# Attention projection of a hybrid decoder step: the branch shares go into the merged tiles ahead of the projection, and the first weight sums move behind the last output block

## The chip, the cores and the metric

One core of a Trainium2 chip runs the whole kernel. The metric is the time on the device in microseconds (us): the median of some runs, and beside it one profiled execution, from which the durations come. Five engines work side by side, each in its own order: PE (TensorE, the matmuls), DVE (VectorE), ACT (ScalarE), POOL (GpSimd) and SP (SyncE, which here only issues DMAs). POOL issues the DMAs that accumulate.

## The reference

One layer of a decoder, for a prompt of 1024 tokens and 8 sample tokens that share the weights. Three branches read the same normalised input, and a gate weighs each of them:

```python
y_a = (sc_b * conv_u) @ w_sc_out
y_b = group_rmsnorm(y_ssd, ssm_norm_w, SSM_GROUPS) @ w_ssm_out
y_c = jnp.einsum('bhlm,bmhd->blhd', probs, mem_v).reshape(bsz, seq, ATTN_DIM) @ w_attn_o
g_a, g_b, g_c = jnp.split(jax.nn.sigmoid(gates), N_BRANCHES, axis=-1)
merged = g_a * y_a + g_b * y_b + g_c * y_c
return merged @ w_merge_o, ...
```

The change concerns the last product of the third branch (`@ w_attn_o`), its gate `g_c`, and the sum `merged`. What follows it is `merged @ w_merge_o`, the residual, and a SwiGLU block.

## The kernel before

Activations lie transposed: a tile has 128 of the 1024 model columns as partitions and the 1032 tokens along its rows. A row of eight such tiles is one activation. Every fp32 product is made of three products of split operands (high by high, high by low, low by high), so every weight block and every activation is first split: ACT casts the high part (`hi`, lines 169, 179, 282, 441), DVE subtracts it from the source for the low part (`lo`, lines 170, 180, 283, 443).

The attention projection works on pairs of output blocks (m = 0, 2, 4, 6; the trace calls them ao0, ao2, ao4, ao6) with a Strassen scheme (`strassen`, line 359). A pair has two raw weight blocks (r1, r2) and seven products of 24 matmuls each (line 295): with the weights A (from r1) the products B11 and B21; with S (sums `sa` of r1 and r2) T1 and nT2; with T (sums `sb`) T3 and B22; with D (the second half of r2) T4. The activations come as seven prepared forms of the attention tiles (`raw8`; names aB11, aT1, ..., aT4; the forms T4 are made last, in `last_aforms`). Three PSUM banks (m0, m1, m2) take the products; ACT copies a result out of its bank (line 380), or DVE combines it with another (lines 351, 429, 431), before the bank is used again. For ao0 and ao2, B11 and B21 are made ahead (`st_head`).

Ahead of the pairs stand the eight output blocks of the second branch (wo20 to wo27, `out_part`, line 1522); the last two are made in halves, and DVE adds to each half a partial sum `yr` loaded by SP (lines 1533, 1543) and multiplies it by its gate (1544). The results go to DRAM as `yg_d` (second branch), and those of the first branch lie in `mg_d`.

In the loop over the pairs (line 1912), `fetch`, called in the middle of `strassen`, loads the gates (line 1925). What is done with the two other shares differs:

- for m = 0 and 2 the gated projection is written to the merged tiles (lines 1941, 1942, 1946), and then four accumulating DMAs of POOL add `yg_d` and, behind these, `mg_d` (line 1952);
- for m = 4 and 6 SP loads `yg_d` into a tile of its own (line 1928), POOL accumulates `mg_d` on it (1929), and DVE adds it to the gated projection (1944, 1945, 1948).

The merged tiles are then split (line 1960) and multiplied by `w_merge_o` (line 2020, tiles `pm`).

The order of the work is made by a planner, which lays the instructions of each engine in a fixed order by the program's order and by what is ready in its own estimate; each engine then works strictly in that order, and waits where something is late. Three devices matter beside that:

- buffers are taken in turn: three for raw weight blocks (tag `raw`), three each for `whi` and `wlo`, five for tiles of the kind `ev` (results, sums, loaded gates), eight for `big` (the attention tiles, then the merged tiles), one for a gate in the pool `fxo`;
- `in_turn` (line 127) keeps the loads of raw blocks, the casts and the subtractions for weights in the program's order;
- `tc.issue_after(x)` keeps an engine's instructions of a block behind x on that engine, without a wait for its end.

Of the kernel before, what the change touches and what calls it, by code (L numbers as in the profile page):

```python
# [9 lines left out]
F32 = mybir.dt.float32  # L10
F32R = mybir.dt.float32r
AF = mybir.ActivationFunctionType
ALU = mybir.AluOpType
# [4 lines left out]
P = 128  # L18
# [3 lines left out]
TT = T + NS  # L22
# [4 lines left out]
KD = D // P  # L27
# [16 lines left out]
def tile_kernel(ctx: ExitStack, tc, a, o):  # L44
    nc = tc.nc
    V, S, G, PE, SY = nc.vector, nc.scalar, nc.gpsimd, nc.tensor, nc.sync

    def f32(t):
        return t.bitcast(F32)
# [21 lines left out]
    def dram(name, shape):  # L71
        return dp.tile(shape, F32, tag=name, name=name)
# [54 lines left out]
    def in_turn(key, ins):  # L127
        if key in prev:
            tc.add_manual_dep(
                ins.ins, prev[key].name,  # L130
                mybir.DependencyInfo(mybir.DependencyClass.NoSync, mybir.DependencyReason.DATA),
                reason="in_turn",
            )
        prev[key] = ins.ins

    loaded = {}

# [35 lines left out]
    def ev_tile(name, shape=(P, TT + 4), dt=F32):  # L173
        return ev.tile(list(shape), dt, tag="ev", name=name)

    def split_act(src, name):
        hi = act_tile("ah", name + "h")
        lo = act_tile("al", name + "l")
        S.copy(hi, src)
        V.tensor_sub(lo, src, f32(hi))  # L180
        return hi, lo
# [67 lines left out]
    def wblock(w, col):  # L249
        return w[:, col : col + P].rearrange("(k p) c -> p k c", p=P)  # L250
# [5 lines left out]
    HS = [slice(0, HT), slice(HT, TT)]  # L256
# [9 lines left out]
    def hv(ps):  # L266
        return ps.rearrange("p n c -> p (n c)")[:, 256 : 256 + HT]

    def halves_of(ps, x, at=0):
        f = hv(ps)  # L270
        for lo, hi in HALF:
            yield f[:, lo:hi], x[:, at + lo : at + hi]

    def st_raw(src, name):
        raw = wp.tile([P, 1024], F32, tag="raw", name=name)
        in_turn("raw", SY.dma_start(raw.rearrange("p (k c) -> p k c", k=KD), src))
        return raw

    def st_split(src, name, n=1024):
        hi = wp.tile([P, 1024], F32R, tag="whi", name=name + "h")  # L280
        lo = wp.tile([P, 1024], F32R, tag="wlo", name=name + "l")
        in_turn("hi", S.copy(hi[:, :n], src))
        in_turn("lo", V.tensor_sub(lo[:, :n], src, f32(hi)[:, :n]))
        return hi, lo

    def st_ps(tag, name):
        return pst[0].tile([P, 2, 512], F32, tag=tag, name=name)

    def st_prod(forms, ps, w, off, f, start):
        for kt in range(4):  # L290
            xh, xl = forms[f][kt]
            ks = slice(off + kt * P, off + (kt + 1) * P)
            for i, (wt, x) in enumerate(((w[0], xh), (w[0], xl), (w[1], xh))):
                for po, xc in halves_of(ps, x):
                    PE.matmul(  # L295
                        po, wt[:, ks], xc, start=(start and kt == 0 and i == 0), stop=(kt == 3 and i == 2),
                        skip_group_check=True,
                    )
# [37 lines left out]
    def st_begin(src1, src2, nm, sums):  # L336
        raw1, raw2 = st_raw(src1, f"{nm}r1"), st_raw(src2, f"{nm}r2")
        wA = st_split(raw1, f"{nm}A")
        sa = sums(f"{nm}sa")
        V.tensor_add(sa[:, :512], raw2[:, :512], raw2[:, 512:])  # L340
        V.tensor_add(sa[:, 512:], sa[:, :512], raw1[:, :512])
        wS = st_split(sa, f"{nm}S")
        return raw1, raw2, sa, wA, wS

    def st_head(wA, forms, nm, o11, tags):

        pa, pc = (st_ps(t, f"{nm}{t}") for t in tags)
        st_prod(forms, pa, wA, 0, "B11", True)
        S.copy(o11, hv(pa))
        st_prod(forms, pc, wA, 512, "B21", True)  # L350
        V.tensor_tensor(o11, hv(pc), o11, op=ALU.add)
        return pa
# [98 lines left out]
    mg_d = dram("mg_d", [KD, P, TT])  # L451
    yr_d = dram("yr_d", [KD, P, TT])
    yg_d = dram("yg_d", [KD, P, TT])
# [34 lines left out]
    with tc.tile_pool(name="p0", bufs=1) as p0, tc.tile_pool(name="pop", bufs=1, space=PSUM) as pop:  # L488
# [30 lines left out]
        for key, src, n in (  # L519
# [13 lines left out]
            while done < n:  # L533
                b, off = divmod(at, P)
                m = min(n - done, P - off)
# [1029 lines left out]
    ins = ((sc_d, a["w_sc_out"][0]), (yb_d, a["w_ssm_out"][0, 0:D]), (yb_d[8:16], a["w_ssm_out"][0, D : 2 * D]), (None, None))  # L1565
# [59 lines left out]
    def big(name):  # L1625
        return ph2[0].tile([P, TT], F32, tag="big", bufs=8, name=name)

    raw8, aforms = [], {}

    def aform(f, kt, src, c=slice(0, HT)):  # L1630
        if kt % 2 == 0 and c.start == 0:
            mk = afx.get(f) or (lambda part, nm: act_tile(part, nm, shape=(P, 2, HT)))
            pair = [mk(part, f"a{f}{kt}{part}") for part in ("ah", "al")]
            aforms.setdefault(f, []).extend(tuple(t[:, i, :] for t in pair) for i in range(2))
        split_to(*(t[:, c] for t in aforms[f][kt]), src)

    afx = {}
    if True:
# [232 lines left out]
            run_next(outs)  # L1871
        wa = [wblock(a["w_attn_o"][0], m * P) for m in range(KD)]
        ev_sums = lambda n: ev_tile(n, (P, 1024))
        begun = st_begin(wa[0], wa[1], "ao0", ev_sums)
        for c in (slice(0, T - HT), slice(T - HT, HT)):
            for kt in range(4):
                b11, b12 = (raw8[kt][:, h][:, c] for h in HS)
# [10 lines left out]
    fxo = fxo_stack.enter_context(tc.tile_pool(name="fxo", bufs=2))  # L1888
    afx["T4"] = lambda part, nm: fxo.tile([P, 2, HT], F32R, tag=part, name=nm)
    oos = [[ev_tile(f"ao0{i}")[:, :TT] for i in range(2)], [ev_tile("ao20")[:, :TT]]]  # L1890
    raw_b = st_raw(wa[2], "ao2r1")
    ta, tb, tc_ = accs
    heads_ = [st_head(begun[3], aforms, "ao0", oos[0][0][:, HS[0]], (ta, tb))]
    wA2 = st_split(raw_b, "ao2A")
    heads_.append(st_head(wA2, aforms, "ao2", oos[1][0][:, HS[0]], (tc_, tb)))

# [6 lines left out]
    def last_aforms():  # L1903
        for kt in range(4):
            aform("B22", kt, raw8[kt + 4][:, HS[1]])
        for kt in range(4):
            t2, b21 = raw8[kt][:, HS[0]], raw8[kt + 4][:, HS[0]]
            V.scalar_tensor_tensor(t2, t2, -1.0, b21, op0=ALU.mult, op1=ALU.subtract)
            aform("T4", kt, t2)

    merged = []
    for m in range(0, KD, 2):
        oo = oos[m // 2] if m < 4 else [big(f"mg{m + i}") for i in range(2)]
        gts, ygs = [], []
        if m == 2:
            oo.append(big("mg3"))
            raw_d = st_raw(wa[3], "ao2r2")
            sa2 = ev_sums("ao2sa")
            V.tensor_add(sa2[:, :512], raw_d[:, :512], raw_d[:, 512:])
            V.tensor_add(sa2[:, 512:], sa2[:, :512], raw_b[:, :512])  # L1920
            begun = raw_b, raw_d, sa2, wA2, st_split(sa2, "ao2S")
        def fetch():
            for i in range(2):
                gts.append((fxo.tile([P, TT], F32, tag="gt", bufs=1, name=f"gt3{m + i}") if i else ev_tile(f"gt3{m + i}"))[:, :TT])
                SY.dma_start(gts[i], gt_d[16 + m + i])
            for i in range(2 if m >= 4 else 0):
                ygs.append(ev_tile(f"yg{m + i}")[:, :TT])
                SY.dma_start(ygs[i], yg_d[m + i])
                G.dma_start(ygs[i], mg_d[m + i], accum_op=ALU.add)

        pa = strassen(
            wa[m], wa[m + 1], aforms, f"ao{m}", ev_sums, lambda: tuple(t[:, c] for t in oo for c in HS),
            begun=begun if m < 4 else None, mid=fetch, hook=None if m else form3,
            after_t3=None if m else last_aforms, head=heads_[m // 2] if m < 4 else None,
        )
        if m == 2:
            accs.clear()
            accs.extend((ta, tb, tc_))
        merged += [big(f"mg{i}") for i in range(2)] if m == 0 else [big("mg2"), oo[1]] if m == 2 else oo
        c1, c0 = HS[1], HS[0]  # L1940
        V.tensor_mul(merged[m], oo[0], gts[0])
        V.tensor_mul(merged[m + 1][:, c1], oo[1][:, c1], gts[1][:, c1])
        if m >= 4:
            V.tensor_add(merged[m], merged[m], ygs[0])
            V.tensor_add(merged[m + 1][:, c1], merged[m + 1][:, c1], ygs[1][:, c1])
        V.scalar_tensor_tensor(merged[m + 1][:, c0], pa, -1.0, gts[1][:, c0], op0=ALU.mult, op1=ALU.mult)
        if m >= 4:
            V.tensor_add(merged[m + 1][:, c0], merged[m + 1][:, c0], ygs[1][:, c0])
        else:
            for src in (yg_d, mg_d):  # L1950
                for i in range(2):
                    G.dma_start(merged[m + i], src[m + i], accum_op=ALU.add)
    fxo_stack.close()
    aux_stack = ExitStack()
    auxp = aux_stack.enter_context(tc.tile_pool(name="aux", bufs=3))
# [4 lines left out]
    mg = [split_act(merged[m], f"mgs{m}") for m in range(KD)]  # L1960
# [164 lines left out]
    for n, (j, j2) in enumerate(pairs):  # L2125
        s1, s2, pa = hidden_pair("g", j, j2)
# [3 lines left out]
        u1, u2, pa = hidden_pair("u", j, j2)  # L2130
# [73 lines left out]
    for part, js in enumerate(([0], [9, 10])):  # L2204
# [6 lines left out]
        begun = st_begin(*down_src(part, 0), f"d{part}0", ev_sums)  # L2211
# [199 lines left out]
```

## Time and profile before

| | us |
|---|---|
| median of 3 runs | 2439.47 (2437.26 to 2442.43) |
| the profiled execution | 2439.55 |
| its span, first to last instruction | 2437.8 |
| PE busy | 2393.3 (98%) |
| DVE busy | 1644.2 (67%) |
| ACT busy | 1113.0 (46%) |
| POOL busy | 116.3 (5%) |

The attention projection begins about 1545 us after the span's start and ends at 1654.45, where the merge product begins. A row of the timeline gives start, duration, engine, line, operation, result and operands, and in brackets how long the engine had been idle before and what released it. A row of the waits gives who waited for whom, the total, the number of times and the longest. A row of a stretch gives the busy time of each engine in it, with the number of instructions, PE's granted clock and how busy the 16 DMA engines were. The trace leaves out buffer numbers, so `mg` is any merged tile, and `yr` any of its kind.

### The profile page before, as it was taken

The page shows a single profiled execution, that of the slowest core. Times are in us where ns is not written, and L with a number is a line of the kernel's source. Part 1 is how long each engine was busy: PE and PEld are TensorE (multiplying, and loading weights), DVE is VectorE, ACT ScalarE, POOL GpSimd, SP SyncE. Part 2 cuts the span into 40 slices and gives each one's busy share as a digit, 9 for nine tenths or more (in the row PEclk, how much of TensorE's full clock was granted, in tenths as well). Part 3 has the DMA queues.
Part 4 walks back from the last instruction along what each step waited for, and adds up shares of the span by engine and source line. Part 5 has one row for each costly group of instructions (what it writes and reads, how often), then busy time and mean ns, then how long its engine had stood idle before and what let it go on. Part 6 is the DMA issues. An engine that isn't in the chain of part 4 may idle for free. (4 is left out here: it accounts for less than half of the span.)

```text
span 2437.8 us, 45645 instructions
## 1 busy us (share of the span) xinstructions
PE 2393.3 (98%) x18860; PEld 2285.6 (94%) x18860; DVE 1644.2 (67%) x2686; ACT 1113.0 (46%) x1792; POOL 116.3 (5%) x175
## 2 busy tenths in 40 slices
PE   8999999999999999999999999889999999999998
PEld 6999999999999999888888887889999999999998
DVE  6744676777777775568687763755777655567965
ACT  6634555455454544656555442333553333343423
POOL 0000000000000000212211000010000000000000
PEclk9999999999999999999999999999999999999999
DMA  6444423444444346669787887496455332355622
GB/s 212 134 155 158 131 89 113 130 139 131 130 151 119 113 122 191 205 226 291 243 292 212 274 316 265 146 224 196 134 178 171 105 109 94 103 169 159 195 85 81
DMA packets 356678, 407.90 MB, mean 167 GB/s; under 512 B 15230, under 2 KB 276462, under 8 KB 356463
## 3 DMA queue, kind: packets, MB, share of 16 engines
q1 hardware_dynamic: 331606, 335.39, 44.8%
q10 hardware_dynamic: 23137, 63.26, 6.8%
q0 software_dynamic: 1728, 6.34, 1.4%
q8 instruction: 148, 2.42, 0.4%
q14 instruction: 59, 0.48, 0.1%
HBM read 288.81 MB, written 116.35 MB: 166 GB/s over the span
## 5 line engine op out<-in xcount | busy, mean ns | idle before, releaser
L1055 ACT ACTIVATE r<-r,acum 128x128 f32<-128x128 f32 x256 | 79.3, 391 | 3.4 <-DMA r<-ac_d 2.5
L844 DVE SCALAR_TENSOR_TENSOR ax<-u,prm,ax 128x1024 f32<-128x1024 f32 x44 | 56.3, 1279 | 0.0
L996 ACT ACTIVATE st<-st,es 128x128 f32<-128x128 f32 x128 | 41.4, 392 | 20.9 <-DMA st<-in_state_ssm_dram 13.5
L1088 POOL TENSOR_TENSOR xdd<-xdt,decst 128x512 f32<-128x512 f32 x32 | 35.2, 1101 | 284.9 <-DVE xdt L1084 279.0
L1082 DVE TENSOR_TENSOR r<-r,cbm 128x1024 f32<-128x1024 f32 x32 | 39.1, 1222 | 4.3 <-ACT r L1057 2.4
L998 DVE SCALAR_TENSOR_TENSOR st<-sr,dts,st 128x128 f32<-128x128 f32 x128 | 40.3, 345 | 0.4
L1107 DVE TENSOR_TENSOR y<-po,ea 128x512 f32<-128x512 f32 x28 | 19.3, 689 | 31.2 <-PE po L1103 31.2
L1124 PE MATMUL pss<-xdd,bT 128*128 128x512 f32 x64 | 34.4, 619 | 2.0 <-ACT bT L1081 1.4
L1002 DVE SCALAR_TENSOR_TENSOR sr<-st,sr 128x128 f32<-128x128 f32 x128 | 35.3, 286 | 1.1
L1111 PE MATMUL py<-r,xdt 128*64 128x128 f32 x512 | 35.0, 279 | 0.0
L1057 ACT ACTIVATE r<-r 128x1024 f32<-128x1024 f32 x32 | 33.8, 1058 | 0.7
L1137 POOL TENSOR_TENSOR s<-s,cdec 128x512 f32<-128x512 f32 x28 | 33.1, 1184 | 0.8 <-DVE s L1130 0.6
L2034 DVE TENSOR_TENSOR x<-pm,xT 128x516 f32<-128x516 f32 x15 | 10.4, 693 | 32.2 <-PE pm L2020 31.2
L1111 PEld LDWEIGHTS py<-r,xdt 128*64 128x64 f32 x512 | 27.3, 136 | 4.4 <-issue 1.0
L1103 PE MATMUL po<-bc,s 128*128 128x128 f32 x224 | 29.6, 275 | 0.0
L1103 PEld LDWEIGHTS po<-bc,s 128*128 128x128 f32 x224 | 28.0, 191 | 1.0
L1689 ACT ACTIVATE pr<-psa,mx 128x256 f32<-128x256 f32 x32 | 14.9, 469 | 29.5 <-DVE mx L1687 29.5
L847 DVE SCALAR_TENSOR_TENSOR ax<-u,prm,ax 128x1032 f32<-128x1032 f32 x22 | 28.3, 1286 | 0.0
L1677 DVE SCALAR_TENSOR_TENSOR kc<-kc,qb 128x256 f32<-128x256 f32 x64 | 23.8, 419 | 6.4 <-DMA qb<-qs_d 6.4
L841 ACT ACTIVATE ax<-u,prm 128x1024 f32<-128x1024 f32 x22 | 27.4, 1246 | 1.2 <-ACT u L923 0.4
L1084 DVE TENSOR_TENSOR xdt<-xp,dtT 128x512 f32<-128x512 f32 x32 | 21.9, 684 | 8.4 <-PE xp L1077 8.4
L1081 ACT COPY bT<-bp 128x128 f32<-128x128 f32 x32 | 8.3, 261 | 38.5 <-DVE cbm L1079 38.5
(9294 smaller groups left out, 9055.9 us busy)
## 6 DMA issues: line engine op xcount, KB each, us to landing
r<-ac_d SPq DMA_DIRECT2D x32, 512.0 KB
gt_d<-G ACTq DMA_DIRECT2D x24, 516.0 KB
gt<-gt_d SPq DMA_DIRECT2D x24, 516.0 KB
xs_d<-ax ACTq DMA_DIRECT2D x22, 516.0 KB
zs<-zs_d SPq DMA_DIRECT2D x16, 516.0 KB
yb_d<-x SPq DMA_DIRECT2D x16, 516.0 KB
in<-yb_d SPq DMA_DIRECT2D x16, 516.0 KB
st<-in_state_ssm_dram SPq DMA_DIRECT2D x32, 256.0 KB
```

Source lines behind the costliest of these rows:

```text
L844: V.scalar_tensor_tensor(acc[:, :T], u[:, j : j + T], w[j], acc[:, :T], op0=ALU.mult, op1=ALU.add)
L996: S.activation(st[:, i], st[:, i], AF.Copy, scale=es[:, g * 4 + i, b : b + 1])
L998: V.scalar_tensor_tensor(st[:, i], rb, dts[:, g * 4 + i, b : b + 1], st[:, i], op0=ALU.mult, op1=ALU.add)
L1002: V.scalar_tensor_tensor(rb, st[:, i], 1.0, rc, op0=ALU.mult, op1=ALU.mult, accum_out=ys[:, g * 4 + i, b : b + 1],)
L1055: S.activation(r[:, j, :], r[:, j, :], AF.Relu, scale=-1.0, bias=acum[:, c, h : h + 1])
L1057: S.activation(r, r, AF.Exp, scale=-1.0)
L1082: V.tensor_tensor(r, r, bc(cbm.unsqueeze(1), [P, HPG, P]), op=ALU.mult)
L1088: G.tensor_tensor(b3(xdd, HPG), b3(xdt, HPG), bc(decst[:, c, hs].unsqueeze(2), [P, HPG, 64]), op=ALU.mult)
L1103: PE.matmul(po[:, t * P : (t + 1) * P], state["s"][:, t * P : (t + 1) * P], bcg[1][:, cs], start=True, stop=True,)
L1111: PE.matmul(py[hp : hp + 64, (h // 2) * P : (h // 2 + 1) * P], xdt[:, h * 64 : (h + 1) * 64], r[:, (h % 2) * 4 + h // 2, :], start=True, s ...
L1124: PE.matmul(pss, bT, xdd, start=True, stop=True)
L1137: G.tensor_tensor(b3(s_new, HPG), b3(state["s"], HPG), bc(cdec[:, c, hs].unsqueeze(2), [P, HPG, 64]), op=ALU.mult,)
```

## The change

The first pair's start is divided. Ahead of the last output block only r1 of ao0 is loaded and split; r2 is loaded behind that block, and its sums S follow the two heads. Result tiles of all pairs are now `ev` tiles, and the merged tiles are made in `shares`: SP loads `yg_d` into the merged tile, POOL accumulates `mg_d` on it. For m = 0 that is called when the last forms are done, for the other pairs in `fetch`; on SP it is kept behind the latest load of a raw weight block. DVE then multiplies the result by its gate in place and adds it to the merged tile, for all four pairs. The two gates of a pair change places between `ev` and `fxo`.

```diff
         prev[key] = ins.ins
+        return ins.ins
...
+    last_raw = [None]
+
     def st_raw(src, name):
         raw = wp.tile([P, 1024], F32, tag="raw", name=name)
-        in_turn("raw", SY.dma_start(raw.rearrange("p (k c) -> p k c", k=KD), src))
+        last_raw[0] = in_turn("raw", SY.dma_start(raw.rearrange("p (k c) -> p k c", k=KD), src))
         return raw
...
-        begun = st_begin(wa[0], wa[1], "ao0", ev_sums)
+        raw_a = st_raw(wa[0], "ao0r1")
+        wA0 = st_split(raw_a, "ao0A")
...
+    raw_c = st_raw(wa[1], "ao0r2")
     raw_b = st_raw(wa[2], "ao2r1")
     ta, tb, tc_ = accs
-    heads_ = [st_head(begun[3], aforms, "ao0", oos[0][0][:, HS[0]], (ta, tb))]
+    heads_ = [st_head(wA0, aforms, "ao0", oos[0][0][:, HS[0]], (ta, tb))]
...
+    def sums_of(raw1, raw2, nm):
+        sa = ev_sums(f"{nm}sa")
+        V.tensor_add(sa[:, :512], raw2[:, :512], raw2[:, 512:])
+        V.tensor_add(sa[:, 512:], sa[:, :512], raw1[:, :512])
+        return sa, st_split(sa, f"{nm}S")
+
+    def shares(ms):
+        for m in ms:
+            merged.append(big(f"mg{m}"))
+            with tc.issue_after(last_raw[0]):
+                SY.dma_start(merged[m], yg_d[m])
+            G.dma_start(merged[m], mg_d[m], accum_op=ALU.add)
+
+    def last_forms_and_shares():
+        last_aforms()
+        shares(range(2))
+
     for m in range(0, KD, 2):
-        oo = oos[m // 2] if m < 4 else [big(f"mg{m + i}") for i in range(2)]
-        gts, ygs = [], []
-        if m == 2:
-            oo.append(big("mg3"))
+        gts = []
+        if m == 0:
+            oo = oos[0]
+            sa0, wS0 = sums_of(raw_a, raw_c, "ao0")
+            begun = raw_a, raw_c, sa0, wA0, wS0
+        elif m == 2:
+            oo = oos[1] + [ev_tile("ao21")[:, :TT]]
             raw_d = st_raw(wa[3], "ao2r2")
-            sa2 = ev_sums("ao2sa")
-            V.tensor_add(sa2[:, :512], raw_d[:, :512], raw_d[:, 512:])
-            V.tensor_add(sa2[:, 512:], sa2[:, :512], raw_b[:, :512])
-            begun = raw_b, raw_d, sa2, wA2, st_split(sa2, "ao2S")
+            sa2, wS2 = sums_of(raw_b, raw_d, "ao2")
+            begun = raw_b, raw_d, sa2, wA2, wS2
+        else:
+            oo = [ev_tile(f"ao{m}{i}")[:, :TT] for i in range(2)]
+            begun = None
+
         def fetch():
             for i in range(2):
-                gts.append((fxo.tile([P, TT], F32, tag="gt", bufs=1, name=f"gt3{m + i}") if i else ev_tile(f"gt3{m + i}"))[:, :TT])
+                gts.append((ev_tile(f"gt3{m + i}") if i else fxo.tile([P, TT], F32, tag="gt", bufs=1, name=f"gt3{m + i}"))[:, :TT])
                 SY.dma_start(gts[i], gt_d[16 + m + i])
-            for i in range(2 if m >= 4 else 0):
-                ygs.append(ev_tile(f"yg{m + i}")[:, :TT])
-                SY.dma_start(ygs[i], yg_d[m + i])
-                G.dma_start(ygs[i], mg_d[m + i], accum_op=ALU.add)
+            if m:
+                shares(range(m, m + 2))
...
-            begun=begun if m < 4 else None, mid=fetch, hook=None if m else form3,
-            after_t3=None if m else last_aforms, head=heads_[m // 2] if m < 4 else None,
+            begun=begun, mid=fetch, hook=None if m else form3,
+            after_t3=None if m else last_forms_and_shares, head=heads_[m // 2] if m < 4 else None,
...
-        merged += [big(f"mg{i}") for i in range(2)] if m == 0 else [big("mg2"), oo[1]] if m == 2 else oo
         c1, c0 = HS[1], HS[0]
-        V.tensor_mul(merged[m], oo[0], gts[0])
-        V.tensor_mul(merged[m + 1][:, c1], oo[1][:, c1], gts[1][:, c1])
-        if m >= 4:
-            V.tensor_add(merged[m], merged[m], ygs[0])
-            V.tensor_add(merged[m + 1][:, c1], merged[m + 1][:, c1], ygs[1][:, c1])
-        V.scalar_tensor_tensor(merged[m + 1][:, c0], pa, -1.0, gts[1][:, c0], op0=ALU.mult, op1=ALU.mult)
-        if m >= 4:
-            V.tensor_add(merged[m + 1][:, c0], merged[m + 1][:, c0], ygs[1][:, c0])
-        else:
-            for src in (yg_d, mg_d):
-                for i in range(2):
-                    G.dma_start(merged[m + i], src[m + i], accum_op=ALU.add)
+        V.tensor_mul(oo[0], oo[0], gts[0])
+        V.tensor_add(merged[m], merged[m], oo[0])
+        V.tensor_mul(oo[1][:, c1], oo[1][:, c1], gts[1][:, c1])
+        V.tensor_add(merged[m + 1][:, c1], merged[m + 1][:, c1], oo[1][:, c1])
+        V.scalar_tensor_tensor(oo[1][:, c0], pa, -1.0, gts[1][:, c0], op0=ALU.mult, op1=ALU.mult)
+        V.tensor_add(merged[m + 1][:, c0], merged[m + 1][:, c0], oo[1][:, c0])
```

## The prediction

> **What bounds the kernel now.** I read the page first, then PE's waits around the attention projection (the four pairs ao0, ao2, ao4, ao6), then the stretches there, and at last each engine's timeline and the queues.
>
> ```profile
> span 2437.8 us, 45645 instructions
> PE 2393.3 (98%) x18860; PEld 2285.6 (94%) x18860; DVE 1644.2 (67%) x2686; ACT 1113.0 (46%) x1792; POOL 116.3 (5%) x175
> ...
> PE ao0m L295 <- DVE yr L1543: 6.0, 2, 5.7
> PE ao2m L295 <- DVE mg L429: 5.6, 1, 5.6
> PE ao6m L295 <- DVE ao6Sl L283: 1.6, 1, 1.6
> PE ao6m L295 <- DVE mg L431: 1.3, 1, 1.3
> ```
>
> PE is the bound nearly everywhere, so only a hole in PE's work can be won. The region has three, which I call A (5.7 us, ahead of ao0), B (5.6 us, in ao2) and C (1.3 and 1.6 us, in ao6). The stretches show what else is full there; the columns after the times are PE, PEld, DVE, ACT and POOL busy, PE's granted clock, the DMA share and GB/s.
>
> ```profile
> 1570.00:1580.00 10.00, 10.00 (x86) 10.00 (x85) 10.00 (x17) 5.80 (x9) 0.00 (x0) 1.00 0.33 107
> 1580.00:1590.00 10.00, 10.00 (x86) 10.00 (x85) 7.83 (x11) 2.54 (x4) 1.89 (x2) 1.00 0.48 118
> 1590.00:1600.00 10.00, 8.49 (x70) 8.09 (x68) 1.62 (x3) 2.11 (x4) 1.72 (x2) 1.00 1.05 247
> 1600.00:1610.00 10.00, 5.91 (x30) 5.91 (x31) 8.15 (x11) 1.76 (x2) 0.85 (x1) 0.66 1.05 274
> ```
>
> VectorE is full up to about 1588 while the DMA engines are half empty; then they are full, VectorE sits idle and PE stops. Hole B, on VectorE, the SP queue and POOL:
>
> ```profile
> 1588.43 0.38 SPq L276 DMA_DIRECT2D ao4r<-in_w_attn_o_dram x1
> 1586.55 1.01 POOL L1952 DMA_DIRECT2D mg<-yg_d  x1 [279.17 <-DVE mg L1941]
> 1595.62 0.86 POOL L1952 DMA_DIRECT2D mg<-mg_d  x1 [6.33 <-DMA mg<-yg_d]
> DMA to landing us min/median/max: 7.7/9.1/9.8
> 1599.80 0.69 DVE L398 TENSOR_TENSOR ao4sa<-ao4r 128x512 f32<-128x512 f32 x1 [8.38 <-DMA ao4r<-in_w_attn_o_dram]
> 1603.35 0.68 DVE L429 TENSOR_TENSOR mg<-mg,ao2m 128x516 f32<-128x516 f32 x1
> 1604.09 0.80 PE L295 MATMUL ao2m<-aT40ah,ao2Dh 128*128 128x256 f32 x2 [5.60 <-DVE mg L429]
> ```
>
> The second weight block of ao4 is asked for at 1588.43, among the accumulating DMAs of mg0 and mg1, and arrives at 1599.8, 11.4 us later. VectorE works in order: L398 waits for that block, and L429, which clears the bank PE needs for T4, stands five instructions behind it. Hole C is of the same kind, with an accumulate as the late one:
>
> ```profile
> 1606.66 0.81 SPq L1928 DMA_DIRECT2D yg<-yg_d x2
> 1611.17 1.11 POOL L1929 DMA_DIRECT2D yg<-mg_d  x1
> 1620.58 1.18 POOL L1929 DMA_DIRECT2D yg<-mg_d  x1
> 1632.24 0.70 DVE L1945 TENSOR_TENSOR mg<-mg,yg 128x516 f32<-128x516 f32 x1 [6.96 <-DMA yg<-mg_d]
> ```
>
> The share of yg5 is issued on POOL only at 1620.58, after the chained accumulates of mg2 and mg3, and L1945 holds VectorE for 6.96 us.
>
> **What the holes are worth.** PE's rows at the borders of the pairs:
>
> ```profile
> 1609.35 0.40 PE L295 MATMUL ao4m<-aB110ah,ao4Ah 128*128 128x256 f32 x2
> 1629.36 0.40 PE L295 MATMUL ao6m<-aB110ah,ao6Ah 128*128 128x256 f32 x2
> 1636.59 0.64 PE L295 MATMUL ao6m<-aT10al,ao6Sh 128*128 128x256 f32 x2
> 1654.45 25.59 PE pm L2020 x213
> ```
>
> The undisturbed pair ao4 takes 1629.36 - 1609.35 = 20.0 us for seven products, 2.86 each. The pair ao6 takes 1654.45 - 1629.36 = 25.1, so C costs 5.1: 2.9 of waiting and 2.2 at the lower clock behind it. In B, T4 runs from 1604.09 to 1609.35, 5.3 us instead of 2.9: B costs 5.6 + 2.4 = 8.0. Here a rule and a row differ. The row at 1636.59 shows a pair of matmuls at 0.64 us, not 0.40, although neither wait of C exceeds 1.6 us. "TensorE: Matmul & The Clock Gate" in the Trainium skill (Part 1, What's actually happening) has the clock fall after an idle window of about 3.4 us; by that, C would be worth 2.9 alone and the ceiling below 2.2 smaller. The row decides, and it also says that a new hole of 2 or 3 us costs about 2.2 more than itself.
>
> **The change, part by part.** *The second ao0 block and its sums move behind the last output block.* Weight splits keep the program's order (in_turn): now the split of the output block wo27 comes behind that of ao0S, which waits for the block ao0r2. With ao0S moved, wo27's split is free to run early.
>
> ```profile
> 1551.52 1.22 DVE L170 TENSOR_TENSOR wo27l<-wo27r,wo27h 128x1024 fp32r<-128x1024 f32 x1
> 1544.45 1.29 DVE L1543 TENSOR_TENSOR yr<-po,yr 128x516 f32<-128x516 f32 x2 [13.92 <-issue]
> 1545.80 0.58 PE L295 MATMUL ao0m<-aB110ah,ao0Ah 128*128 128x256 f32 x1 [5.71 <-DVE yr L1543]
> 1539.66 0.43 SPq L1533 DMA_DIRECT2D yr<-yr_d x1
> ```
>
> PE can then take wo27 straight after wo26. Its first half has an empty bank, its second needs the first of the two L1543, done at about 1545.1. So A stays: it hangs on the yr load issued at 1539.66, which is not touched, and PE gains 0.7 us at most (1545.8 against 1545.1), nothing if the order stays. The block ao0r2, its two adds (0.68 each) and split (1.22) have the whole of wo27 and two heads (four products, 11.4 us) before T1 wants them. They cost nothing while that cover holds; without it their 2.6 us plus a cast of 1 us would stand in front of T1.
>
> *The merged shares.* Twelve accumulating DMAs become eight and four plain loads become eight; the bytes stay. In the window 1540 to 1680 the two queues show:
>
> ```profile
> q1 hardware_dynamic: 20112, 19.52, 45.0%
> q0 software_dynamic: 1728, 6.34, 24.1%
> ```
>
> An accumulate fills all engines for 24.1% of 140 / 12 = 2.8 us, a plain 0.53 MB load for 45.0% of 140, by 19.52 MB, x 0.53 = 1.7. The queues lose 4 x 1.1 = 4.4 us of work. More matters when they start: the merged tiles are free as soon as the last forms have read the attention tiles.
>
> ```profile
> 1574.96 0.68 DVE L443 TENSOR_TENSOR aT40al<-at,aT40ah 128x516 fp32r<-128x516 f32 x1
> 1584.76 1.23 DVE L1941 TENSOR_TENSOR mg<-ao,gt 128x1032 f32<-128x1032 f32 x1
> 1585.91 0.69 DVE L1942 TENSOR_TENSOR mg<-ao,gt 128x516 f32<-128x516 f32 x1
> 1587.72 0.68 DVE L328 SCALAR_TENSOR_TENSOR ao2sb<-ao2sa,ao2r 128x512 f32<-128x512 f32 x1
> 1589.60 1.22 DVE L283 TENSOR_TENSOR ao2Tl<-ao2sb,ao2Th 128x1024 fp32r<-128x1024 f32 x1 [1.19 <-ACT ao2Th L282]
> 1592.39 0.40 PE L295 MATMUL ao2m<-aB220ah,ao2Th 128*128 128x256 f32 x2
> 1635.86 1.23 DVE L1944 TENSOR_TENSOR mg<-mg,yg 128x1032 f32<-128x1032 f32 x1
> ```
>
> So yg0 and yg1 can be asked for at about 1576, ten microseconds before the first accumulate of now, into queues a third full. For ao4 and ao6 the shares no longer wait for an ev buffer (1606.66 above) nor behind mg2 and mg3 on POOL. C's cause goes: I take its 5.1 back in full, with 0 as the other end should VectorE still meet a late share.
>
> For B, the accumulates of mg0 and mg1 are done or nearly so when ao4r2 is asked for, and mg2 and mg3 no longer form chains of two. Four accumulates at 2.8 us are 11.2 us of engine work; if half of them are over by 1588, the 11.4 us of ao4r2 fall by up to 5.6, and with the shorter wait the clock may hold. I take 6 of B's 8.0; the ends are 0 (the same bytes in the way) and 8.0.
>
> *What VectorE gets more.* ao0 and ao2 gain an add of 1.23 and two of 0.69 each, 2.6 us a pair. In ao2 they meet time in which VectorE idles (8.38). In ao0 it has none, and ao2Tl ends at 1590.8 for a product starting at 1592.39: a margin of 1.6 us. wo27l (1.22) leaves this stretch for idle time. Also the adds now wait for the shares: yg0 asked for at 1576, landed 3.9 us later (SP's 1606.66 to POOL's move on at 1610.55 is such a load), plus 9.1 for the accumulate, gives 1589, where VectorE could add at 1586. If the program's order holds, ao2sb and ao2T stand 3 us plus the adds behind that, ao2Tl ends about 4 us later, PE waits some 3 us and loses 2.2 of clock, 5 together; if the planner lets ao2sb pass, nothing. Ends 0 and 5; I take 3, between them since I cannot see the new order.
>
> **Sum.** 0.7 + 5.1 + 6 - 3 = 8.8 us off the profiled run. That run took 2439.55 (1.75 beside its span), 0.1 from the median of 2439.47, so I forecast 2430.7. What a measurement of this kernel can tell from no change is about 0.2%, 4.9 us.
>
> **Rivals.** *All is won:* no new wait and B closed: 0.7 + 5.1 + 8.0 = 13.8, 2425.7. For it speaks the idle DMA time before 1586, against it VectorE's full rows to 1588.
>
> *Hole B stays.* The weight block still shares the engines with POOL's accumulates, since the new order only holds back SP's loads: only C and the start are won and the 3 us paid, 2.8 off, 2436.7. The rows of 1586.55 to 1595.62 speak for it: four accumulates flew while SP's block took 11.4 us. "DMA: Bandwidth & Descriptors" of the Trainium skill (Issuing engines are not separate DMA queues) says that transfers of all issuing engines interleave on the same 16 engines. By that an order on SP alone does not protect the block; the 11.4 us agree.
>
> *Slower: the shares become VectorE's bound.* Place: the first add of ao0, with ao2sb behind it. When the last share of ao0 lands at time L, what follows is an add, the product with its add, two ao2sb sums, the cast and the split, some 5.6 us, so PE gets ao2T at L + 5.6 and loses L + 5.6 - 1591.7 plus 2.2. It eats the 13.8 at L = 1597.7; if B stays as well, the 5.8 left is eaten at 1589.7. L would be that late if yg1 were asked for only at 1587, behind a load on SP that waits for its buffer (3.9 + 9.1 = 13.0). At L = 1600 and B staying, the loss is 16.1 against 5.8: 10.3 slower, 2449.9. Against it: the SP rows show transfers of later pairs issued when ready, not held behind earlier blocked ones.
>
> *The change doesn't do what it says:* the planner asks for the shares no earlier than today's accumulates, holes as before, the adds in their shadow: 2439.5.
>
> **How the numbers follow.** Forecast 0.4, all won 0.17, B stays 0.15, inert 0.08, slower 0.2. Faster by over 0.2% (below 2434.6): the first two and a little of the third, 0.6. Within 0.2%: the rest of the third, inert and the mild end of slower, 0.2. Slower by over 0.2%: 0.2, the slower rival and combinations of it, less its mild end. The range runs from all won with 1.7 to spare, 2424.0, to 2445.0, half way into the slower rival.
>
> **What would show it.** Right: plain loads of yg_d on SP into mg at about 1576; the first accumulate on POOL before 1582; no 5.6 us wait of PE at T4 of ao2, none at T1 of ao6; wo27 on PE ahead of ao0's B11. Wrong: PE's waits naming ao2Tl or an mg add, VectorE idle for "mg<-mg_d", or ao4r still 11 us under way. The merge products (pm) should start about 9 us earlier than 1654.45.

## The result, and the profile after

The changed kernel takes 2436.06 us, median of 20 runs (2431.87 to 2439.0), against 2440.01 of the kernel before on the same chips (20 runs, 2436.99 to 2445.74). The ratio is 0.9981, interval 0.9974 to 0.9988: about 4.6 us faster, where 8.8 were forecast. The profiled execution took 2438.7.

PE's waits from 1530 to 1700 us, changed kernel (the wait ahead of wo26, the same in both kernels, left out):

```profile
PE ao2m L298 <- ACT ao2Sh L285: 9.9, 1, 9.9
...
PE ao0m L298 <- ACT ao0Sh L285: 1.0, 1, 1.0
PE ao0m L298 <- DVE yr L1546: 0.7, 1, 0.7
PE ao0m L298 <- DVE ao0Sl L286: 0.6, 1, 0.6
PE ao2m L298 <- DVE ao L354: 0.5, 1, 0.5
PE ao2m L298 <- DVE ao2Al L286: 0.4, 1, 0.4
```

The long waits of before are gone: 5.7 at yr (A), 5.6 in ao2 (B), 1.3 and 1.6 in ao6 (C). In their place stands one new wait of 9.9 us, for the weights ao2S, and a row of short ones. The borders of the blocks and pairs on PE's timeline, first in the kernel before, then in the changed one:

```profile
1526.89 0.50 PE L242 MATMUL po<-b00h,wo26h 128*128 128x256 f32 x2 [1.32 <-DVE yr L1558]
...
1586.68 0.41 PE L295 MATMUL ao2m<-aT10ah,ao2Sh 128*128 128x256 f32 x2
...
1654.29 0.40 PE L2020 MATMUL pm<-mgs0h,wm00h 128*128 128x256 f32 x2
```

```profile
1530.34 0.51 PE L243 MATMUL po<-b00h,wo26h 128*128 128x256 f32 x2 [1.32 <-DVE yr L1561]
...
1543.38 0.40 PE L243 MATMUL po<-b00h,wo27h 128*128 128x256 f32 x2
1549.07 0.40 PE L243 MATMUL po<-b00h,wo27h 128*128 128x256 f32 x2
...
1612.12 0.40 PE L298 MATMUL ao4m<-aB110ah,ao4Ah 128*128 128x256 f32 x2
...
1632.08 0.40 PE L298 MATMUL ao6m<-aB110ah,ao6Ah 128*128 128x256 f32 x2
...
1652.04 0.40 PE L2039 MATMUL pm<-mgs0h,wm00h 128*128 128x256 f32 x2
```

The changed kernel's first row starts 3.45 us later than that of the kernel before. The instructions ahead of it are the same in the same order, so that is the variation of one execution, and what follows is measured by the **region**: from the first matmul of wo26 to the first of the merge product. It is 127.4 us before (1526.89 to 1654.29) and 121.7 after, 5.7 less. The pair ao6 takes 19.96 us, as undisturbed as ao4: C is gone. At 1543.38 the first half of wo27 runs straight behind wo26, in an empty bank, and the second half follows without a wait: that is how A went.

Where the new wait comes from, on the timelines of SP, POOL, DVE and PE:

```profile
1577.65 2.14 SPq L1928 DMA_DIRECT2D mg<-yg_d  x4
1581.86 1.01 POOL L1929 DMA_DIRECT2D mg<-mg_d  x1 [273.15 <-DVE ao L432]
1583.09 0.87 POOL L1929 DMA_DIRECT2D mg<-mg_d  x1 [0.23 <-DVE aT42al L446]
1585.63 0.68 DVE L1920 TENSOR_TENSOR ao2sa<-ao2r 128x512 f32<-128x512 f32 x1
1588.72 1.23 DVE L1967 TENSOR_TENSOR mg<-mg,ao 128x1032 f32<-128x1032 f32 x1 [2.40 <-DMA mg<-mg_d]
1592.85 0.69 DVE L1969 TENSOR_TENSOR mg<-mg,ao 128x516 f32<-128x516 f32 x1 [2.90 <-DMA mg<-mg_d]
1593.46 0.69 DVE L1970 SCALAR_TENSOR_TENSOR ao<-ao0m,gt 128x516 f32<-128x516 f32 x1
1594.07 0.68 DVE L1921 TENSOR_TENSOR ao2sa<-ao2sa,ao2r 128x512 f32<-128x512 f32 x1
1595.93 0.80 PE L298 MATMUL ao2m<-aT10ah,ao2Sh 128*128 128x256 f32 x2 [9.86 <-ACT ao2Sh L285]
```

The sum ao2sa has two instructions. The first, L1920, ran at 1585.63. Between it and the second, L1921, the planner has put both adds of ao0 that need shares (L1967, L1969) and L1970, which needs the end of T4 of ao0. The shares came 6.9 and 9.8 us after POOL had asked for them, VectorE waited 2.40 and 2.90 us, and PE, which wanted T1 of ao2 at 1586.07, got it at 1595.93.

The block behind hole B, by contrast, came quickly:

```profile
1597.06 0.68 DVE L331 SCALAR_TENSOR_TENSOR ao2sb<-ao2sa,ao2r 128x512 f32<-128x512 f32 x1
1597.77 0.38 SPq L279 DMA_DIRECT2D ao4r<-in_w_attn_o_dram  x1
1602.47 0.69 DVE L401 TENSOR_TENSOR ao4sa<-ao4r 128x512 f32<-128x512 f32 x1 [1.72 <-DMA ao4r<-in_w_attn_o_dram]
```

That is 4.7 us against 11.4 before. But it was also asked for late: 11.7 us behind the point at which PE could have begun T1 of ao2 (1586.07), where it was 1.7 us in the kernel before (1588.43 and 1586.68). With three buffers in turn, this block takes the one of ao2's first block, whose last reader is the second sum T (L328 before, L331 now); in every traced run the request goes out 0.7 us after that sum's start. The new wait held that sum up. By 1597.77 the accumulates of mg0 to mg2 had landed, and that of mg3 had 0.8 us to go (asked for at 1586.43, 12.1 us under way).

### The profile page after: what moved, and what is told of

It reads as the page before. It is cut to its first block, busy times and chain, and to the rows that moved or that the text cites. A ratio compares the mean times of both kernels' runs of the same rounds, so it can differ in the third digit from the quotient of the medians.

```text
span 2437.0 us, 45647 instructions
## 1 busy us (share of the span) xinstructions
PE 2388.5 (98%) x18860; PEld 2281.0 (94%) x18860; DVE 1647.6 (68%) x2692; ACT 1112.9 (46%) x1792; POOL 112.9 (5%) x171
## 5 line engine op out<-in xcount | busy, mean ns | idle before, releaser
L999 ACT ACTIVATE st<-st,es 128x128 f32<-128x128 f32 x128 | 41.3, 392 | 18.4 <-DMA st<-in_state_ssm_dram 16.2
L2053 DVE TENSOR_TENSOR x<-pm,xT 128x516 f32<-128x516 f32 x15 | 10.4, 693 | 32.0 <-PE pm L2039 32.0
```

The lines of the kernel that those rows point to most:

```text
L999: S.activation(st[:, i], st[:, i], AF.Copy, scale=es[:, g * 4 + i, b : b + 1])
```

## The experiments

Region is from the one profiled execution of each kernel, ratio from the timed runs against the kernel before on the same chip, with its 95% interval.

| kernel | region, us | ratio | longest hole of PE |
|---|---|---|---|
| before | 127.4 | 1 | A, B, C |
| changed | 121.7 | 0.9981 (0.9974 to 0.9988) | T1 of ao2, 9.9 |
| block alone | 125.1 | 0.9991 (0.9981 to 1.0001) | T4 of ao2, 3.1; T1 of ao2, 2.6 |
| shares alone | 123.3 | 0.9987 (0.9978 to 0.9996) | T1 of ao2, 6.1; A, 6.0 |
| pair 0 as before | 128.0 | 1.0004 (0.9995 to 1.0014) | T4 of ao2, 10.5 |
| one share left out | 117.2 | 0.9963 (0.9951 to 0.9975) | T1 of ao2, 5.0 |
| no order on SP | 126.0 | 1.0012 (0.9997 to 1.0026) | T1 of ao2, 10.7 |
| pair 2 held | 122.7 | 0.9980 (0.9969 to 0.9990) | T1 of ao2, 10.5 |
| sums S first | 120.0 | 0.9975 (0.9964 to 0.9985) | T3 of ao2, 6.8 |
| sums S first, pair 2 held | 122.8 | 0.9978 (0.9969 to 0.9987) | T3 of ao2, 6.4 |
| all sums first | 123.0 | 0.9978 (0.9970 to 0.9987) | T3 of ao2, 9.4 |
| and ao4's blocks first | 117.0 | 0.9962 (0.9949 to 0.9975) | T3 of ao2, 3.3 |
| and a cast behind a copy | 119.9 | 0.9968 (0.9957 to 0.9979) | T3 of ao4, 4.7 |

The theory: from about 1579 to 1605 the DMA engines are full but for a dip about 1598, and PE stops where an engine that works in order has something that PE needs behind an instruction that waits for a transfer. The rival: VectorE is full, and the order of its work alone makes the hole. The fences of the experiments hold rows of the timelines of PE, VectorE and, where they matter, SP, POOL and ScalarE, each of the kernel that its paragraph is about.

**The moved block alone** (kernel before, with only the second ao0 block and its sums moved):

```diff
-        begun = st_begin(wa[0], wa[1], "ao0", ev_sums)
+        raw_a = st_raw(wa[0], "ao0r1")
+        wA0 = st_split(raw_a, "ao0A")
...
+    raw_c = st_raw(wa[1], "ao0r2")
```

> The kernel before with only the second ao0 block and its sums moved behind the last output block; shares as before. Theory 1 (the shares make the new hole: DVE waits for them with ao2's sums behind it): hole A goes (8.0 us with its clock), B (8.0) and C (5.1) stay, no hole at T1 of ao2; 8 us faster, ratio 0.9967. Rival (the new order alone makes it: ao2's second sum stands behind the gated product that needs T4 of ao0): a hole of some 4 us and 2 us of clock at T1 of ao2 with no share waited for; 2 us faster, ratio 0.999.

```profile
1560.32 0.47 PE L295 MATMUL ao0m<-aB210ah,ao0Ah 128*128 128x256 f32 x2 [0.73 <-DVE yr L1543]
1591.28 0.80 PE L295 MATMUL ao2m<-aT10ah,ao2Sh 128*128 128x256 f32 x2 [2.63 <-ACT ao2Sh L282]
1607.59 0.60 PE L295 MATMUL ao2m<-aT40ah,ao2Dh 128*128 128x256 f32 x2 [3.13 <-DVE mg L429]
```

A is closed by the block alone, since of the wait for yr 0.73 us is left. B is there, shorter because PE, held at T1, comes to T4 later. And T1 of ao2 waits 2.63 us though VectorE waits for no share here: the rival holds for that part, and its ratio of 0.999 is the one measured.

**The shares alone** (changed kernel, ao0's block and sums ahead as before):

```diff
-        raw_a = st_raw(wa[0], "ao0r1")
-        wA0 = st_split(raw_a, "ao0A")
+        begun = st_begin(wa[0], wa[1], "ao0", ev_sums)
```

> The kernel after with both ao0 blocks and their sums ahead of the last output block, as before; shares as after. Theory 1: A stays, B and C go (13.1), but the adds of ao0 wait for the shares and hold ao2's weights as in the kernel after, 12 us; 1 us faster, ratio 0.9996. Rival: ao2's sums come early in this order, so there is no hole at T1; the adds hold ao2sb at most, 3 to 5 us and 2 of clock at T3; 6 to 8 us faster, ratio 0.997.

```profile
1595.74 0.77 PE L298 MATMUL ao2m<-aT10ah,ao2Sh 128*128 128x256 f32 x2 [6.06 <-DVE ao L434]
1594.30 0.70 DVE L1965 TENSOR_TENSOR mg<-mg,ao 128x516 f32<-128x516 f32 x1 [5.33 <-DMA mg<-mg_d]
```

A stays, B and C go. The hole at T1 of ao2 is there as well, by another road: ao2S is ready, but the bank is cleared by L434, which stands behind the add that waits 5.33 us for a share. The hole is half of what the theory expected, where the rival expected none.

**Pair 0 added by DMA as before** (changed kernel otherwise):

```diff
         last_aforms()
-        shares(range(2))
...
+        if m == 0:
...
+                    G.dma_start(merged[i], src[i], accum_op=ALU.add)
```

> The kernel after with the pair ao0 added as before (gated product written to the merged tiles, four accumulating DMAs behind it), the other three pairs by shares. Theory 1: no DVE instruction waits for a share in ao0; what is left at T1 of ao2 is the wait for T4, 4 us and 2 of clock; if hole B stays closed, 8 us faster than before more than after gives: 21 less 6 less 3 = 12 faster, ratio 0.995; if the accumulates of ao0 beside ao4's block open B again (8 us), 4 faster, ratio 0.998. Rival: the hole at T1 of ao2 stays near 10 us, ratio 0.998 or above.

```profile
1586.43 0.50 PE L298 MATMUL ao2m<-aT10ah,ao2Sh 128*128 128x256 f32 x2 [2.63 <-ACT ao2Sh L285]
1586.47 0.38 SPq L279 DMA_DIRECT2D ao4r<-in_w_attn_o_dram  x1
1607.40 0.69 DVE L401 TENSOR_TENSOR ao4sa<-ao4r 128x512 f32<-128x512 f32 x1 [17.93 <-DMA ao4r<-in_w_attn_o_dram]
1610.60 0.80 PE L298 MATMUL ao2m<-aT40ah,ao2Dh 128*128 128x256 f32 x2 [10.47 <-DVE ao L432]
```

Without adds that wait for shares, T1 of ao2 waits 2.63 us, as with the block alone. The large hole is B again: ao4's second block is 20.9 us under way, where it meets four accumulates and the early shares of pair 2. This run does not tell which of two differences closes B in the changed kernel, the early shares of pair 0 or the late request: here the block is also asked for only 2.7 us behind the point at which PE could begin T1 of ao2, not 11.7. The run with all sums first, below, bears on that.

**One share left out.**

```diff
-            G.dma_start(merged[m], mg_d[m], accum_op=ALU.add)
+            m < 2 or G.dma_start(merged[m], mg_d[m], accum_op=ALU.add)
```

> The changed kernel without the two accumulating DMAs of the first branch on mg0 and mg1; that share is missing from those two merged tiles. VectorE's order is the changed kernel's but for two swaps of an add with a sum. Theory (VectorE's adds wait for shares that the DMA engines bring late, and ao2's second sum stands behind them): no wait of VectorE for a share in pair ao0, the hole at T1 of ao2 falls from 9.9 us to the 2.6 us that the order alone cost when only the block was moved, so some 7 us less, about 2429 us. Rival (the hole is VectorE's load and order, the shares only happen to land then): the hole stays over 7 us, 2435 to 2437 us.

```profile
1593.11 0.80 PE L298 MATMUL ao2m<-aT10ah,ao2Sh 128*128 128x256 f32 x2 [4.98 <-ACT ao2Sh L285]
```

No add waits for a share, and the hole is 4.98 us: between the two expectations. The 2.4 us above the 2.6 of order (the block alone) come with the new adds and two swaps in VectorE's order. Most of the 9.9 us of the changed kernel can be told from its own rows: the two adds ahead of L1921 take some 1.8, and VectorE waits 2.40 and 2.90 for transfers; with the 2.6 of order, which another kernel showed, that is 9.7.

**No order on SP** (the loads of shares not kept behind the last raw block; only SP's order differs):

```diff
-            with tc.issue_after(last_raw[0]):
+            with nullcontext():
```

> The changed kernel without keeping the share loads behind the last raw weight block on SP; only SP's order differs: the loads for mg4 to mg7 stand ahead of the second weight block of ao4. Theory (queue order on SP protects that block): the block is up to 3.4 us (two plain loads at 1.7) later than its 4.7 us, or SP itself is held by tiles that are not free and asks for the block late; a hole at T4 of ao2 comes back, 2438 to 2445 us. Rival (transfers go out as their tiles come free, whatever SP's order, and the clause does nothing): 2435.5 to 2436.5 us.

```profile
1585.28 5.67 SPq L1928 DMA_DIRECT2D mg<-yg_d  x4
1597.71 0.38 SPq L279 DMA_DIRECT2D ao4r<-in_w_attn_o_dram  x1
1609.04 0.69 DVE L401 TENSOR_TENSOR ao4sa<-ao4r 128x512 f32<-128x512 f32 x1 [8.34 <-DMA ao4r<-in_w_attn_o_dram]
1612.25 0.50 PE L298 MATMUL ao2m<-aT40ah,ao2Dh 128*128 128x256 f32 x2 [1.69 <-DVE ao L432]
```

The clause matters: without it the shares of pairs 4 and 6 go out ahead of ao4's second block, which, asked for at nearly the same time, then takes 11.3 us instead of 4.7, and no gain is left in the timed runs: the theory's range of 2438 to 2445 holds with 2444.5. These twelve runs spread from 2437.4 to 2453.5 us, and the traced one took 2440.4, so the trace shows less than the median has lost. I had held that an order on SP alone does not protect the block.

**Pair 2's shares held back** behind the load of gt32 (only SP's order differs):

```diff
-                SY.dma_start(gts[i], gt_d[16 + m + i])
+                last_raw[m != 2 or i] = SY.dma_start(gts[i], gt_d[16 + m + i]).ins
```

> The changed kernel; SP's loads of the second branch's share for mg2 and mg3 kept behind the load of the gate gt32, nothing else in any engine's order differs. Theory (the DMA engines' queue sets the landing: two plain loads of 1.7 us and then two accumulates of 2.8 us stand in the way of mg0 and mg1): the share of mg1 lands 3 to 4 us earlier, the hole at T1 of ao2 falls from 9.9 to about 6 us, 2432 to 2433 us. Rival (the same bytes only meet another reader): the held shares now fly with the second weight block of ao4 and its wait comes back as a hole at T4 of ao2; 2436 to 2439 us.

```profile
1595.08 0.86 POOL L1929 DMA_DIRECT2D mg<-mg_d  x1 [11.35 <-DVE ao L1970]
1582.86 0.88 POOL L1929 DMA_DIRECT2D mg<-mg_d  x1 [0.20 <-DVE aT42al L446]
1593.22 0.70 DVE L1969 TENSOR_TENSOR mg<-mg,ao 128x516 f32<-128x516 f32 x1 [3.83 <-DMA mg<-mg_d]
```

The share of mg1 lands 10.4 us after POOL's request, not earlier than the 9.8 of the changed kernel. Pair 2's accumulates are out of its way, since POOL asks for the first at 1595.08, and still it comes no sooner: that part of my theory fails. Pair 2's plain loads, held only until 1585.87, still fly beside it, and whether they delay it stays open. No hole opens at T4 of ao2, as the rival had it.

**Sums S first** (ao2's second block, its sums S and their split ahead of ao0's last forms):

```diff
     def last_forms_and_shares():
+        d2.append(st_raw(wa[3], "ao2r2"))
+        d2.extend(sums_of(raw_b, d2[0], "ao2"))
         last_aforms()
```

> The kernel after with ao2's second block, its two S sums and their split asked for ahead of the last forms of ao0, so ahead of the merged adds on DVE. Theory 1: the 9.9 us at T1 of ao2 go; ao2sb stays behind the adds, so some 5 us and 2 us of clock come at T3; 5 us faster than after, 9 to 10 faster than before, ratio 0.996. Rival (the place in the order does not matter, the late shares decide): as the kernel after, ratio 0.998.

```profile
1596.50 0.70 DVE L1972 TENSOR_TENSOR mg<-mg,ao 128x516 f32<-128x516 f32 x1 [2.40 <-DMA mg<-mg_d]
1597.72 0.68 DVE L330 TENSOR_TENSOR ao2sb<-ao2r,ao2r 128x512 f32<-128x512 f32 x1
1600.79 0.80 PE L298 MATMUL ao2m<-aT30ah,ao2Th 128*128 128x256 f32 x2 [6.75 <-ACT ao2Th L285]
```

T1 no longer waits; T3 does, since now the sums T (L330) stand behind the adds. The gain is some 6 us, less than the 9 to 10 of theory 1, and its interval overlaps that of the changed kernel. With pair 2's shares held back as well:

> The variant with ao2's sums ahead of ao0's last forms, and with the shares of mg2 and mg3 held as in the other run. Theory: the hole at T3 of ao2 (6.8 us there) falls to about 3 us, 2431 to 2432 us, the best so far. Rival: the hole moves to T4 of ao2 behind the second weight block of ao4, 2434 to 2437 us.

```profile
1609.98 0.70 DVE L1972 TENSOR_TENSOR mg<-mg,ao 128x516 f32<-128x516 f32 x1 [4.83 <-DMA mg<-mg_d]
1613.01 0.50 PE L298 MATMUL ao4m<-aT10ah,ao4Sl 128*128 128x256 f32 x2 [2.45 <-DVE ao4Sl L286]
```

The hole at T3 is 0.4 us shorter (6.4), and the share held back makes a hole of its own, in ao4, where neither expectation had it. Against the sums S alone the intervals overlap.

**All sums first** (sums T too, in the tile of the gate gt, and the clearing of T4's bank ahead of the adds):

```diff
         V.tensor_mul(oo[0], oo[0], gts[0])
-        V.tensor_add(merged[m], merged[m], oo[0])
+        if m == 0:
...
+            ready2 = raw_b, d2[0], d2[1], d2[2], st_sums2(raw_b, d2[0], d2[1], "ao2", sb2)
...
+        V.tensor_add(merged[m], merged[m], oo[0])
```

> The variant with ao2's sums S ahead of ao0's last forms, and in addition its sums T (in the tile of the gate gt) and T4's clearing of the bank ahead of ao0's adds, so that PE's T1 to T4 of ao2 need nothing that stands behind an add but the splits ao2T (behind mg0's add alone) and ao2D. The shares are asked for as there. Theory (a hole opens where VectorE's order has something that PE needs behind a transfer under way): no wait of PE at T1 or T3 of ao2 above 1.5 us, the region from wo26 to the merge product falls from the 120.0 us of that variant by its 6.8 us hole and some 2 us of clock to about 111, 2426 us, if the second weight block of ao4 comes by 1601. Rival (the DMA engines are full and the hole only moves on): the next thing that a transfer holds is L401, which waits for that block and has L432 behind it; asked for at about 1590 and 11 to 15 us under way, it lands at 1601 to 1605 and opens 2 to 5 us and the clock's 2 at T4 of ao2, region 114 to 117, 2430 to 2433 us.

```profile
1585.54 3.34 SPq L279 DMA_DIRECT2D ao4r<-in_w_attn_o_dram  x2
1603.41 0.80 PE L298 MATMUL ao2m<-aT30ah,ao2Th 128*128 128x256 f32 x2 [9.38 <-ACT ao L383]
1601.82 1.04 ACT L285 CAST ao4Ah<-ao4r 128x1024 fp32r<-128x1024 f32 x1 [11.19 <-DMA ao4r<-in_w_attn_o_dram]
1604.04 0.68 DVE L401 TENSOR_TENSOR ao4sa<-ao4r 128x512 f32<-128x512 f32 x1
```

VectorE holds PE up no longer (the one wait for ao2Tl is 1.1 us), and the hole is as long as ever: now ScalarE stands at the cast of ao4's first block, asked for at 1585.54 and 16 us under way, with the copy L383 behind it that clears the bank for T3. Neither expectation had named that place. ao4's second block, the one behind B, is asked for at about 1588.5 here, some 8 us sooner in the region than in the changed kernel, and is some 15 us under way (L401 reads it at 1604.04), though pair 0's shares are as early as in the changed kernel. So the early shares alone do not bring that block in time; the late request has its part in the 4.7 us. Whether a late request alone would do was not tried.

**And ao4's blocks first** (asked for ahead of the shares of mg2 and mg3):

```diff
+            if m == 2:
+                raws4.extend((st_raw(wa[4], "ao4r1"), st_raw(wa[5], "ao4r2")))
             if m:
                 shares(range(m, m + 2))
...
+        if m == 2:
+            wA4 = st_split(raws4[0], "ao4A")
```

> As the variant with all of ao2's sums ahead, and ao4's two weight blocks asked for on SP ahead of the shares of mg2 and mg3, which then go out only behind the loads of ao2's... of the gates gt32 and gt33, at about 1593. Theory: the second block of ao4 meets two accumulates instead of four, lands before 1600, no hole at T4 of ao2, region about 111 us, 2426 us. Rival (what is asked for later is late): the shares of mg2 and mg3 land after 1612 and hold VectorE ahead of ao4's sums T or the split ao4S, a hole of 3 to 6 us in ao4, 2431 to 2435 us.

```profile
1585.16 3.29 SPq L279 DMA_DIRECT2D ao4r<-in_w_attn_o_dram  x2
1593.02 1.85 SPq L1928 DMA_DIRECT2D mg<-yg_d  x4
1594.38 1.04 ACT L285 CAST ao4Ah<-ao4r 128x1024 fp32r<-128x1024 f32 x1 [4.17 <-DMA ao4r<-in_w_attn_o_dram]
```

The first block lands some 7 us earlier, the hole at T3 of ao2 is 3.31 us, and the kernel takes 2432.91 us: about 9.3 us less than before (interval 6.1 to 12.5), twice the gain of the change. The blocks are asked for when they were in the version before (1585.16 against 1585.54); what changed is that the shares of mg2 and mg3 now go out at 1593 and not beside them. The time is in the rival's range, the hole not where the rival had it. With the next one it is the best complete version here.

**And the cast behind the copy** on ScalarE:

```diff
-            wA4 = st_split(raws4[0], "ao4A")
+            with tc.issue_after(last_put[0]):
+                wA4 = st_split(raws4[0], "ao4A")
```

> As the best variant so far (all of ao2's sums ahead, ao4's blocks ahead of the shares of mg2 and mg3), with one thing more: on ScalarE the cast ao4Ah, which waited 4.17 us for the first block of ao4 there, is kept behind the copy L383 that clears the bank for T3 of ao2. Theory: the 3.3 us hole at T3 and the clock's share behind it go, the region falls from 117.0 to 112 or 113 us, about 2428.5 us. Rival (the hole moves on again): the shares of mg2 and mg3, which held VectorE 0.9 and 1.4 us there, now hold it 4 to 5 us ahead of ao4's sums T, a hole of 2 to 4 us at T3 of ao4, 2431 to 2433 us.

```profile
1609.00 1.24 DVE L1983 TENSOR_TENSOR mg<-mg,ao 128x1032 f32<-128x1032 f32 x1 [6.75 <-DMA mg<-mg_d]
1616.69 0.80 PE L298 MATMUL ao4m<-aT30ah,ao4Th 128*128 128x256 f32 x2 [4.70 <-ACT ao L383]
```

The hole at T3 of ao2 is gone and a hole of 4.70 opens at T3 of ao4, behind an add that waits 6.75 us for the share of mg2. The rival was right, but for a hole longer than its 2 to 4 us: PE runs up to the next late transfer. Nothing is gained over the version before it, and the two intervals overlap.

## Why the prediction was half right

The direction held, and so did C's cause. Three terms of the sum were mis-sized, in opposite directions, and one of them came for another reason than mine; that they nearly met is luck.

- **"A stays" was wrong** (0.7 forecast). I let the yr load of 1539.66 decide and left out how long the first half of wo27 takes: it goes to an empty bank, ran from 1543.38 to 1549.07, and covers the wait. A's 5.7 and the clock behind it went. Against that, "They cost nothing" was wrong too: with the block moved, short waits of 0.73, 0.51, 0.39, 0.96 and 0.56 us stand in ao0 and ao2 (3.15 together), nearly the same in the kernel with the block alone. From wo26 to where T1 of ao2 could start PE took 59.8 us before (1526.89 to 1586.68) and 55.7 after (1530.34 to 1586.07): 4.1 instead of 0.7.
- **B: 6 forecast, 8.4 won, by another road.** From T1 of ao2 to ao4 PE took 22.7 us before (1586.68 to 1609.35), where five products of 2.86 are 14.3, and no wait of PE at T4 is left. I had the accumulates of mg0 and mg1 done or nearly so when the block is asked for at 1588. At that time none had landed: mg0's came at 1588.7, mg1's at 1592.85. The new wait put the request off to 1597.77, and then the block took 4.7 us; asked for at 1588.5 with all sums first, it took 15. So the runs point to the late request as what my reason lacked, though none has it alone, and the 8.4 won here and the loss below hang together: that this term came near is luck. The rival that B stays had the nearest number, 2436.7 for 2436.06, and that is luck as well, since it kept B's 8.0 and paid only 3. Its reason is half right: a large wait at T4 of ao2 comes back with pair 0's adds left to POOL (10.5 us), a small one without the order on SP (1.7). "DMA: Bandwidth & Descriptors" of the Trainium skill (Issuing engines are not separate DMA queues) says that all issuers' transfers interleave on the same engines; the 20.9 us in the run with pair 0 as before agree. From it I concluded that an order on SP does not protect the block, and the run without that order (11.3 us for the block instead of 4.7) refutes the conclusion.
- **C: 5.1 forecast, 5.0 won.** The row at 1654.45, from which I took 5.1, lies 0.16 us behind the first matmul of the merge product (1654.29).
- **The new wait: 3 forecast, 9.9 and 1.9 of clock measured** (ao2 from 1595.93 to 1612.12 is 16.2 for five products of 2.86). This is the step that failed. The mechanism was named, the place was not. I had the sums T behind the adds, with T3 waiting; the planner put the second half of the sums S there, which PE wants two products earlier. And I let one landing time, 1589, stand for both shares: mg0's came at 1588.7, mg1's at 1592.85, 4.1 us later, though POOL had asked for it only 1.2 us after.

By the region 4.1 + 8.4 + 5.0 - 11.8 = 5.7; the timed runs show 4.6. The forecast gain of 8.8 was above what came: the gain of 0.19% lies just within the 0.2% to which I gave a chance of 0.2. Of the signs named, those of "right" all came but the start of the merge product, and of those of "wrong" VectorE's waits for "mg<-mg_d". The slower rival's mechanism was at work, with its L at 1592.85, short of the 1597.7 at which it would have decided.

The rule from "TensorE: Matmul & The Clock Gate" of the Trainium skill (Part 1, What's actually happening), an idle window of about 3.4 us, disagrees again: with the block alone the clock fell behind a wait of 2.63 us. The stretch behind that wait (columns as in the prediction):

```profile
1592.00:1594.00 2.00, 2.00 (x11) 2.00 (x10) 2.00 (x3) 0.97 (x2) 0.00 (x0) 0.50 1.02 219
```

## What to carry to other kernels

Where the DMA engines are full, closing one hole lets the faster engine run into the next late transfer; price a change by the whole row of transfers, and ask of each instruction that waits for one what PE needs behind it on that engine, on ScalarE as well as VectorE. Ask also what puts a request off: a block that came quickly may have been asked for late, because a buffer came free late. The version that gained most kept transfers that are needed later out of the way of the blocks that PE needs next; the orders of the adds alone, without that, were not told apart from the change by the timed runs. When work is fused into an engine that runs in order, look up what the order has put behind it that PE needs next.

## What the runs showed of the hardware

Two accumulating DMAs of 516 KB, asked for 1.2 us apart for pair 0, took 6.8 and 9.7 us to land. The two of pair 6, asked for 1.3 us apart near the end of the region, took 6.7 and 7.9:

```profile
DMA to landing us min/median/max: 6.7/7.3/7.9
```

The landing of one 512 KB weight block, ao4's second, ranged from 4.7 us (changed kernel) over 11.4 (before) to 20.9 (pair 0 as before), by when it was asked for and what else was under way. The clock's cost behind a hole did not grow with its length here: 1.9 us behind 9.9, 2.4 behind 5.6 (B), 2.0 behind 1.3 and 1.6 (C). The granted clock fell to 0.50 behind one wait of 2.45 us (sums S first, pair 2 held, 1614 to 1616) and stayed at 1.00 behind one of 1.69 (no order on SP, 1612 to 1616).
